# Layer 0 opens with two feature blocks over nine column chunks; w_mod products queue behind the splits

## The chip, the cores and the metric

The kernel runs on one core of one Trainium2 chip. The time is that of one execution on the device, in microseconds (us), and of several executions the median is given.

## What is computed

A trunk of two layers works on 256 tokens with 2048 features. Each layer normalises its input, scales and shifts it by numbers that come from the condition `c` through the matrix `w_mod`, multiplies it by the wide matrix `w_in`, runs retention and latent attention on the pieces, merges them by gates, multiplies by `w_out` and adds the result. Cut to what matters here:

```python
c_act = jax.nn.silu(c)
mod = c_act @ w_mod + b_mod                       # (1, 6144) from a (2048, 6144) matrix, for each layer
shift, scale, gate = jnp.split(mod, 3, axis=-1)
h = rms_norm(x, g_norm) * (1.0 + scale[:, None, :]) + shift[:, None, :]
proj = h @ w_in                                   # (256, 2048) x (2048, D_IN)
```

Everything is in 32-bit floats.

## The kernel before

The 2048 features are 16 blocks of 128, and a block of the normalised, scaled and shifted input `h` lies with its features on the partitions and the 256 tokens along the free axis. A product with a matrix goes in chunks. A chunk is one transfer of 512 KB, two feature blocks by 512 columns. SyncE (SP) issues it into one of five `wst` buffers (`load`, L233). ScalarE (ACT) writes a rounded copy of it and VectorE (DVE) the remainder, into one of three `whl` buffers (`split_into`, L240 to L242). TensorE (PE) then multiplies high by high, high by low and low by high (`chunk`, L262 to L273). A chunk of the first four columns is 24 matmuls of 256 columns, one of the others 12 matmuls of 512. The function `load_split` (L246) does load and split, and gives the split a raised priority for the scheduler, which orders the instructions of each engine's queue.

The numbers `scale` and `shift` come from `w_mod`. Except at the very start VectorE makes these products: for each row block of `w_mod` it multiplies the tile by a column of `cact` and adds it to an accumulator (`mod_rows`, L341 to L346), and TensorE only sums over the partitions at the end (`mod_finish`, L356). A list `background` holds these steps, and `bg` (L417) takes some of them at each `load_split`, by a rate. In `first_products` they go through `mod_pair` with two `ring` buffers, one step for each transfer of 512 KB; later, in `mod_slice`, through the `wst` buffers that the weights use as well.

Layer 0 opens in `start` (L494), whose instructions on TensorE, VectorE and ScalarE stand in an order written by hand. The input comes in four transfers, then 16 transfers of `w_mod` bring scale and shift for the first four feature blocks, first all eight of scale, then all eight of shift, each 256 rows by 512 columns. TensorE transposes the input and multiplies the scale rows (L528); VectorE adds up the shift rows. When both are done `h` is made for four blocks (L541 to L545).

The function `first_products` (L581) then goes over groups of feature blocks, four groups of four in layer 0. In each group it goes over 14 column chunks of 512 (rq and rk, n 0 to 3; rv, n 4 to 7; rg, n 8 to 11; the first gate, n 12 and 13) and adds the group's part to what stands there: the first part is copied out of PSUM by ScalarE (L604), each later one is added by VectorE (L606). Beside a group the background makes scale and shift of the next group. The rate is set such that the last step is taken 8 loads before the group's end (`SPARE`), in layer 1 three loads before (`SPARE1`). At the start of the next group `make_h` turns them into `h`.

Line numbers are those of the kernel before.

## Time and profile before

| | us |
|---|---|
| median of 3 executions | 2107.25 |
| lowest and highest of them | 2105.28, 2107.37 |
| the profiled execution, whole | 2107.54 |
| its span in the profile | 2105.8 |
| TensorE busy | 2045.3 |
| VectorE busy | 1505.9 |
| ScalarE busy | 1060.1 |

The whole time of the profiled execution is 1.7 us longer than its span. A busy engine has an instruction in work; a matmul's end is modelled, so that back-to-back matmuls overlap in the rows. PEclk is TensorE's granted clock, as a share of full speed. DMA is the mean busy share of the 16 DMA engines, GB/s is what they moved.

### The profile page before, as it was taken

What the parts mean: (1) busy time and instruction counts of PE and PEld (TensorE: products, weight loads), DVE (VectorE), ACT (ScalarE), POOL (GpSimd) and SP (SyncE); (2) the same over time, 40 slices, a digit from 0 to 9 for tenths busy, and PEclk for the clock granted to TensorE, in tenths of its full rate; (3) what the DMA queues carried; (4) which work ended last, traced back from release to release, by engine and by line L of the source; (5) the groups of instructions that cost most, each with busy time, mean ns of one, the idle gap of its engine ahead of it and who ended that gap; (6) DMA issues with size and microseconds to landing.
All of it is one profiled execution on the core that took longest, in us unless ns stands there. A gap on an engine that the chain in (4) does not pass through costs nothing. (4 is left out here: it accounts for less than half of the span.)

```text
span 2105.8 us, 31895 instructions
## 1 busy us (share of the span) xinstructions
PE 2045.3 (97%) x12410; PEld 1806.7 (86%) x12414; DVE 1505.9 (72%) x2258; ACT 1060.1 (50%) x1489; POOL 0.2 (0%) x4
## 2 busy tenths in 40 slices
PE   7999999999999999999999999999999999999998
PEld 4887888997789998778999779889878999988887
DVE  5789887777777786666577776557866777765564
ACT  4554355654356665334454454446544666644453
POOL 0000000000000000000000000000000000000000
PEclk9999999999999999999999999999999999999999
DMA  8988866566766667776558976665667666666672
GB/s 315 310 283 274 293 190 199 165 196 228 263 203 194 186 196 250 242 242 216 181 167 304 313 256 184 196 186 156 196 220 231 184 193 186 216 221 189 192 243 91
DMA packets 263511, 460.60 MB, mean 219 GB/s; under 512 B 18464, under 2 KB 68032, under 8 KB 263360
## 3 DMA queue, kind: packets, MB, share of 16 engines
q1 hardware_dynamic: 263360, 458.57, 68.4%
q8 instruction: 97, 1.59, 0.3%
q14 instruction: 54, 0.44, 0.1%
HBM read 456.41 MB, written 2.10 MB: 218 GB/s over the span
## 5 line engine op out<-in xcount | busy, mean ns | idle before, releaser
L241 ACT ACTIVATE whl<-wst 128x1024 fp32r<-128x1024 f32 (+1 forms) x708 | 706.9, 1006 | 770.4 <-PE acc L273 634.9
L242 DVE TENSOR_TENSOR whl<-wst,whl 128x1024 fp32r<-128x1024 f32 (+1 forms) x708 | 811.6, 1156 | 267.2 <-ACT whl L241 264.0
L270 PE MATMUL acc<-whl,h 128*128 128x512 f32 x2048 | 513.6, 391 | 0.9 <-DVE rv L606 0.7
L270 PEld LDWEIGHTS acc<-whl,h 128*128 128x128 f32 x2048 | 381.6, 188 | 79.8 <-issue 1.7
L270 PE MATMUL acc<-h,whl 128*128 128x256 f32 x2432 | 331.0, 287 | 8.6 <-ACT h L241 3.8
L270 PEld LDWEIGHTS acc<-h,whl 128*128 128x128 f32 x2432 | 310.0, 194 | 12.5 <-ACT h L241 5.0
L273 PE MATMUL acc<-whl,h 128*128 128x512 f32 x1024 | 281.8, 395 | 8.5 <-DVE whl L242 8.1
L270 PE MATMUL acc<-whl,z 128*128 128x512 f32 x1024 | 256.7, 392 | 3.8 <-ACT whl L241 3.8
L346 DVE SCALAR_TENSOR_TENSOR macc<-wst,cact,macc 128x512 f32<-128x512 f32 x180 | 135.0, 750 | 140.9 <-DMA wst<-in_w_mod 138.8
L273 PEld LDWEIGHTS acc<-whl,h 128*128 128x128 f32 x1024 | 188.8, 188 | 53.9 <-DVE whl L242 16.9
L270 PEld LDWEIGHTS acc<-whl,z 128*128 128x128 f32 x1024 | 192.8, 189 | 44.7 <-ACT whl L241 4.5
L273 PE MATMUL acc<-h,whl 128*128 128x256 f32 x1216 | 175.1, 284 | 0.0
L273 PEld LDWEIGHTS acc<-h,whl 128*128 128x128 f32 x1216 | 159.1, 193 | 0.1
L273 PE MATMUL acc<-whl,z 128*128 128x512 f32 x512 | 139.8, 395 | 13.2 <-DVE whl L242 13.1
L346 DVE SCALAR_TENSOR_TENSOR tmp<-ring,cact,tmp 128x512 f32<-128x512 f32 x150 | 112.0, 751 | 51.4 <-DMA ring<-in_w_mod 49.9
L273 PEld LDWEIGHTS acc<-whl,z 128*128 128x128 f32 x512 | 95.2, 189 | 39.2 <-DVE whl L242 20.3
L270 PE MATMUL acc<-c,whl 128*128 128x256 f32 x640 | 102.7, 289 | 1.0 <-DVE ma L643 1.0
L270 PEld LDWEIGHTS acc<-c,whl 128*128 128x128 f32 x640 | 86.8, 191 | 1.3 <-ACT q L241 1.2
L270 PE MATMUL acc<-m,whl 128*128 128x256 f32 x512 | 67.3, 283 | 0.0
L270 PEld LDWEIGHTS acc<-m,whl 128*128 128x128 f32 x512 | 64.0, 192 | 0.1
L270 PE MATMUL acc<-whl,m 128*128 128x512 f32 (+1 forms) x256 | 56.5, 365 | 0.0
L273 PE MATMUL acc<-c,whl 128*128 128x256 f32 x320 | 56.0, 283 | 0.0
(259 smaller groups left out, 1889.7 us busy)
## 6 DMA issues: line engine op xcount, KB each, us to landing
wst<-in_w_in SPq DMA_DIRECT2D x416, 512.0 KB, 4.5
wst<-in_w_mod SPq DMA_DIRECT2D x96, 512.0 KB, 4.3
ring<-in_w_mod SPq DMA_DIRECT2D x80, 512.0 KB, 5.5
wst<-in_w_ret_proj SPq DMA_DIRECT2D x64, 512.0 KB, 4.8
wst<-in_w_mla_proj SPq DMA_DIRECT2D x64, 512.0 KB, 4.6
wst<-in_w_out SPq DMA_DIRECT2D x64, 512.0 KB, 3.7
wst<-in_w_ukv SPq DMA_DIRECT2D x32, 512.0 KB, 3.8
wst<-in_w_uq SPq DMA_DIRECT2D x32, 384.0 KB, 4.0
```

Of the source, the lines that this page charges most:

```text
L241: A.activation(hi, src, AF.Copy)
L242: V.tensor_tensor(lo, src, hi.bitcast(F32), ALU.subtract)
L270: T.matmul(o, x, y, start=start and i == 0, stop=False, skip_group_check=True)
L273: T.matmul(o, x, y, start=False, stop=stop, skip_group_check=True)
L346: V.scalar_tensor_tensor(acc, w[:, k, :], cact[:, k0 + k : k0 + k + 1], acc, ALU.mult, ALU.add)
```

## The change

`GROUPS[0]` becomes (0,2), (2,2), (4,4), (8,4), (12,4): the first group of four blocks is cut into two of two. In the new first group only nine of the 14 column chunks are made (`FIRST`), so the second group makes those nine for two blocks and the other five for four. `start` fetches `w_mod` for two blocks only, in eight transfers of 512 rows by 256 columns, scale and shift by turns; behind them the first three chunks of `w_in`, then the eight transfers of `w_mod` for the second two blocks with a chunk of `w_in` after every two. The products of these second blocks become the background of the new first group. The scale products on TensorE stand between the transposes and behind them. `h` is made with the scale inside the activation, and one more VectorE instruction for each block. Everywhere in the kernel the `w_mod` products are queued on VectorE behind the last split that was traced before them (`behind_splits`), and `load` and `mod_fetch` are kept on SyncE in the order of the program. The spare loads are 2, 3, 8, 8, 8 in layer 0 and 3, 3 in layer 1, as before there.

```diff
-GROUPS = ((0, 4), (4, 4), (8, 4), (12, 4)), ((0, 8), (8, 8))
+GROUPS = ((0, 2), (2, 2), (4, 4), (8, 4), (12, 4)), ((0, 8), (8, 8))
+FIRST = 9
-SPARE1 = 3
-SPARE = 8
+SPARE = (2, 3, 8, 8, 8), (3, 3)
 def load(src, nk, n, t=None):
-        DMA.dma_start(v, src.rearrange("(k p) n -> p k n", p=P))
+        tc.keep_in_program_order(DMA.dma_start(v, src.rearrange("(k p) n -> p k n", p=P)))
+    def behind_splits():
+        return tc.issue_after(last_split[-1].ins) if last_split else nullcontext()
 def load_split(src, nk, n, early=False):
-        w = load(src, nk, n)
+        w = loaded.pop(0) if loaded else load(src, nk, n)
-            split_into(hi, lo, w)
+            last_split.append(split_into(hi, lo, w))
 def mod_pair(l, kg, ng, fetched=None):
-                mod_rows(acc[i], mod_fetch(room[used[0] % len(room)], l, kg + 16 * i, k0, ng), k0, nd)
+                if fetched:
+                    w = fetched[i, k0]
+                else:
+                    used[0] += 1
+                    w = mod_fetch(ring()[used[0] % RING], l, kg + 16 * i, k0, ng)
+                with behind_splits():
+                    mod_rows(acc[i], w, k0, nd)
 def mod_slice(l, m0, k0):
-        mod_rows(macc, w, k0, 2)
+        with behind_splits():
+            mod_rows(macc, w, k0, 2)
 def start():
-        ws = {(i, k): mod_fetch(quarter("wmod"), 0, 16 * i, k, ng) for i in (1, 0) for k in range(0, KT, nd)}
+        steps = [(i, k) for k in range(0, KT, nd) for i in (1, 0)]
+        ws = {(i, k): mod_fetch(quarter("wmod"), 0, 16 * i, k, ng) for i, k in steps}
+        loaded.extend(load(src, 2, 512) for src in first[:HP])
+        later = {}
+        for n, (i, k) in enumerate(steps):
+            later[i, k] = mod_fetch(quarter("wmod"), 0, ng + 16 * i, k, ng)
+            if n % 2:
+                loaded.append(load(first[HP + n // 2], 2, 512, quarter("wst") if HP + n // 2 >= WP else None))
+            turns = {4: 0, 6: nd}
             for pair in range(KT // 2):
+                if pair in turns:
+                    scale_rows(turns[pair])
...
             for k0 in range(0, KT, nd):
                 mod_rows(acc, ws[0, k0], k0, nd)
+            prepared.append(load_split(first[0], 2, 512, early=True))
             A.activation(row[0:1, :], pr[0:1, : ng * P], AF.Copy)
+            mod_sum(0, 0, ng, [acc], ones[:, 0:1])
             mod_sum(0, 16, ng, [row[0:1, :]], ones[0:1, 0:1])
             make_amul(0, 0, ng)
...
+                A.activation(hi, xh0[:, k, :], AF.Identity, bias=shift, scale=scale)
+                V.tensor_scalar(xh0[:, k, :], xh0[:, k, :], scale, shift, ALU.mult, ALU.add)
+                V.tensor_tensor(lo, xh0[:, k, :], hi.bitcast(F32), ALU.subtract)
 def first_products(l, hh, r, u, second):
+            if n1 == 2:
+                todo, steps, columns = [second], 9, FIRST
+            else:
+                todo, steps, columns = [mod_pair(l, k, 4) for k in range(k1, k1 + n1, 4)], 17, COLUMNS
-            rate[0] = len(background) / (sum(kg + ng - k for k in upto) // 2 - (SPARE, SPARE1)[l])
-            for n in range(COLUMNS):
+            rate[0] = len(background) / (sum(kg + ng - k for k in upto[:columns]) // 2 - len(prepared) - SPARE[l][i])
+            for n in range(columns):
```

## Rows read from the trace of the kernel before

**Rows 1.** The page, part 1: busy us, share of the span, instructions by engine.
```profile
PE 2045.3 (97%) x12410; PEld 1806.7 (86%) x12414; DVE 1505.9 (72%) x2258; ACT 1060.1 (50%) x1489; POOL 0.2 (0%) x4
```

**Rows 2.** Windows: stretch, length, busy us by engine, PEclk, DMA share, GB/s.
```profile
30.00:40.00 10.00, 6.46 (x25) 3.49 (x24) 9.14 (x18) 2.44 (x4) 0.00 (x0) 0.85 1.05 387
```

**Rows 3.** Timeline of the start: start us, duration us, engine, line, what [idle before].
```profile
19.07 14.27 PE L528 MATMUL aux<-wmod,cact 128*1 128x512 f32 x32
19.18 0.38 ACT L333 ACTIVATE r<-aux 128x256 f32<-128x256 f32 x1 [0.26 <-PE aux L331]
22.02 0.89 ACT L230 ACTIVATE sin_t<-angle,cst 128x256 f32<-128x256 f32 x2
24.33 0.49 DVE L344 TENSOR_SCALAR extra<-wmod,cact 128x512 f32<-128x512 f32 x1 [3.44 <-DMA wmod<-in_w_mod]
35.17 1.06 ACT L241 ACTIVATE whl<-wst 128x1024 fp32r<-128x1024 f32 x1 [1.21 <-DMA wst<-in_w_in]
39.76 3.88 PE L270 MATMUL acc<-h,whl 128*128 128x256 f32 x16 [0.87 <-ACT h L544]
44.53 0.64 PE L270 MATMUL acc<-h,whl 128*128 128x256 f32 x4
```

**Rows 4.** Windows of the groups of layer 0: first, second, third.
```profile
39.70:123.60 83.90, 81.22 (x457) 69.93 (x457) 63.22 (x78) 49.31 (x70) 0.00 (x0) 0.98 0.89 300
123.60:207.40 83.80, 82.17 (x456) 69.74 (x457) 75.03 (x100) 35.48 (x41) 0.00 (x0) 0.98 0.84 275
207.40:288.40 81.00, 79.59 (x457) 67.88 (x456) 73.54 (x96) 34.58 (x38) 0.00 (x0) 1.00 0.84 275
```

**Rows 5.** Timeline, TensorE in the first group: two neighbours of each kind of chunk.
```profile
50.29 2.08 PE L270 MATMUL acc<-h,whl 128*128 128x256 f32 x16
...
53.17 2.08 PE L270 MATMUL acc<-h,whl 128*128 128x256 f32 x16
...
72.87 1.98 PE L270 MATMUL acc<-whl,h 128*128 128x512 f32 x8
...
75.59 1.98 PE L270 MATMUL acc<-whl,h 128*128 128x512 f32 x8
```

**Rows 6.** Waits of the whole span: engine, line, awaited: us, times, longest.
```profile
PE acc L273 <- DVE whl L242: 21.1, 25, 1.8
...
DVE macc L346 <- DMA wst<-in_w_mod: 138.8, 74, 6.3
```

**Rows 7.** Timeline in layer 0's last stage: one product ahead of a split.
```profile
861.00 1.06 ACT L241 ACTIVATE whl<-wst 128x1024 fp32r<-128x1024 f32 x1 [1.52 <-PE acc L273]
862.55 0.75 DVE L346 SCALAR_TENSOR_TENSOR macc<-wst,cact,macc 128x512 f32<-128x512 f32 x1 [1.65 <-DMA wst<-in_w_mod]
863.22 1.22 DVE L242 TENSOR_TENSOR whl<-wst,whl 128x1024 fp32r<-128x1024 f32 x1
864.50 1.20 PE L273 MATMUL acc<-whl,h 128*128 128x512 f32 x4 [1.70 <-DVE whl L242]
```

**Rows 8.** Windows: a stall of TensorE and what follows; rows of 1 KB.
```profile
500.00:516.00 16.00, 10.85 (x46) 8.13 (x46) 13.50 (x28) 4.24 (x6) 0.00 (x0) 0.68 0.71 240
...
2057.00:2058.00 1.00, 1.00 (x6) 0.84 (x5) 1.00 (x1) 0.00 (x0) 0.00 (x0) 1.00 1.01 358
```

**Rows 9.** VectorE by line and shape, 0 to 330 us: count, busy us, mean ns.
```profile
L346 DVE SCALAR_TENSOR_TENSOR tmp<-ring,cact,tmp 128x512 f32<-128x512 f32 x90 | 66.9, 750 | 25.4 <-DMA ring<-in_w_mod 24.7
L606 DVE TENSOR_TENSOR qk<-qk,acc 128x512 f32<-128x512 f32 x24 | 15.6, 684 | 1.4 <-PE acc L273 1.4
...
L545 DVE SCALAR_TENSOR_TENSOR h<-xh,mod,h 128x256 fp32r<-128x256 f32 x4 | 1.7, 483 | 0.6 <-ACT h L544 0.6
```

**Rows 10.** Timeline: last product, first matmul of the second group, a pair of additions.
```profile
108.72 1.54 DVE L346 SCALAR_TENSOR_TENSOR tmp<-ring,cact,tmp 128x512 f32<-128x512 f32 x2 [0.31 <-DMA ring<-in_w_mod]
...
123.65 0.50 PE L270 MATMUL acc<-h,whl 128*128 128x256 f32 x2 [1.48 <-ACT h L241]
...
177.93 1.28 DVE L606 TENSOR_TENSOR rv<-rv,acc 128x512 f32<-128x512 f32 x2
```

More of the change, by code (lines that the diff above doesn't have):

```diff
@@ L230, in rotary_tables, with load @@
             A.activation(sin_t[:, n], a[:, n * S : (n + 1) * S], AF.Sin, scale=cst[:, K_INV + 2 + n : K_INV + 3 + n])
-    def load(src, nk, n):
-        t = wp.tile([P, 1024], F32, name="wst", tag="wst")
+    def load(src, nk, n, t=None):
+        t = wp.tile([P, 1024], F32, name="wst", tag="wst") if t is None else t
         v = t[:, : nk * n].rearrange("p (k n) -> p k n", k=nk)
-        DMA.dma_start(v, src.rearrange("(k p) n -> p k n", p=P))
+        tc.keep_in_program_order(DMA.dma_start(v, src.rearrange("(k p) n -> p k n", p=P)))
         return v
@@ L387, in mod_fetch, with mod_pair @@
         nd = 1024 // n
-        DMA.dma_start(w, w_mod[l, k0 * P : (k0 + nd) * P, m0 * P : m0 * P + n].rearrange("(k p) n -> p k n", p=P))
+        src = w_mod[l, k0 * P : (k0 + nd) * P, m0 * P : m0 * P + n]
+        tc.keep_in_program_order(DMA.dma_start(w, src.rearrange("(k p) n -> p k n", p=P)))
         return w
-    def mod_pair(l, kg, ng):
+    def mod_pair(l, kg, ng, fetched=None):
         acc = [tmp_tile()[:, : ng * P] for _ in range(2)]
@@ L512, in start, with scale_rows @@
             y = rsqrt_small(v, 2)
+            pr = aux_tile()
+            def scale_rows(k0):
+                for k in range(k0, k0 + nd):
+                    T.matmul(pr[0:1, : ng * P], cact[:, k : k + 1], ws[1, k0][:, k - k0, :], start=k == 0, stop=k == KT - 1)
+            turns = {4: 0, 6: nd}
             for pair in range(KT // 2):
+                if pair in turns:
+                    scale_rows(turns[pair])
                 ps = aux_tile()
@@ L524, in start @@
             next(rotary, None)
-            pr = aux_tile()
+            for k0 in range(2 * nd, KT, nd):
+                scale_rows(k0)
             for k0 in range(0, KT, nd):
-                for k in range(nd):
-                    T.matmul(pr[0:1, : ng * P], cact[:, k0 + k : k0 + k + 1], ws[1, k0][:, k, :], start=k0 + k == 0,
-                             stop=k0 + k == KT - 1)
-            for k0 in range(0, KT - nd, nd):
                 mod_rows(acc, ws[0, k0], k0, nd)
+            prepared.append(load_split(first[0], 2, 512, early=True))
             A.activation(row[0:1, :], pr[0:1, : ng * P], AF.Copy)
+            mod_sum(0, 0, ng, [acc], ones[:, 0:1])
             mod_sum(0, 16, ng, [row[0:1, :]], ones[0:1, 0:1])
             make_amul(0, 0, ng)
-            mod_rows(acc, ws[0, KT - nd], KT - nd, nd)
-            for k in range(ng):
-                V.tensor_scalar(xh0[:, k, :], xh0[:, k, :], amul[0][:, k : k + 1], None, ALU.mult)
-            first = [w_in[0, k0 * P : (k0 + 2) * P, n : n + 512] for n in (C_RQ, C_RK) for k0 in range(0, ng, 2)]
-            prepared.append(load_split(first[0], 2, 512, early=True))
-            mod_sum(0, 0, ng, [acc], ones[:, 0:1])
             for k in range(ng):
                 hi, lo = hh.block(k)
-                shift = mods[0][:, k : k + 1]
-                A.activation(hi, xh0[:, k, :], AF.Identity, bias=shift)
-                V.scalar_tensor_tensor(lo, xh0[:, k, :], shift, hi.bitcast(F32), ALU.add, ALU.subtract)
+                scale, shift = amul[0][:, k : k + 1], mods[0][:, k : k + 1]
+                A.activation(hi, xh0[:, k, :], AF.Identity, bias=shift, scale=scale)
+                V.tensor_scalar(xh0[:, k, :], xh0[:, k, :], scale, shift, ALU.mult, ALU.add)
+                V.tensor_tensor(lo, xh0[:, k, :], hi.bitcast(F32), ALU.subtract)
             prepared.extend(load_split(src, 2, 512, early=True) for src in first[1:HP])
-        return r, hh
+        return r, hh, mod_pair(0, ng, ng, later)
     def scaled(l, n):
@@ L589, in first_products @@
         for i, (kg, ng) in enumerate(groups):
-            if l == 0 and i == 1:
+            if l == 0 and i == 2:
                 vectors(1)
@@ L615, in layer @@
         if l == 0:
-            r, hh = start()
+            r, hh, second = start()
         else:
-            hh = Pairs("h")
-        tiles = first_products(l, hh, r, u)
+            hh, second = Pairs("h"), None
+        tiles = first_products(l, hh, r, u, second)
         zz = Pairs("z")
```

13 lines of the change are left out of this document (6 added, 7 removed).

## The prediction, on record before the run

> **What bounds the kernel now.** I read the page's first part, then the windows, the waits, and last the timeline where the windows show a hole. The page's first part says that TensorE is busy 97% of the span [rows 1], so only two kinds of time can be won: time before its main work starts, and stalls in it. The windows show the first: from 30 to 40 us the transfers run at 387 GB/s while TensorE is busy for 6.46 of 10 us [rows 2], and the timeline of the start shows why this is a wait. VectorE's first shift product starts at 24.33, on the landing of the 13th of 20 transfers of 512 KB (four of input, eight of scale, then this first of shift); the first weight chunk, the 21st, is taken up by ScalarE at 35.17; the first main matmul starts at 39.76 [rows 3]. Eight transfers lie between the first two, so one takes (35.17 - 24.33) / 8 = 1.355 us. The start is bound by 8 MB of `w_mod` that stands ahead of the first weight.
>
> The windows of the groups show what comes next. Group one takes 83.9 us with VectorE busy for 63.2, group two 83.8 with VectorE busy for 75.0, group three 81.0 with 73.5 [rows 4]. TensorE sets their length: neighbours of one kind lie 53.17 - 50.29 = 2.88 us apart for the narrow chunk and 75.59 - 72.87 = 2.72 for the wide one [rows 5], so 8 and 20 of them in a group make 23.0 + 54.4 = 77.4 us. But VectorE is a close second.
>
> The waits show the other kind: 25 waits of TensorE, 21.1 us, for the remainder of a split, and 138.8 us in which VectorE stands at a `w_mod` product whose transfer has not landed [rows 6]. The timeline joins the two [rows 7]: ScalarE has the high part ready at 862.06 (861.00 + 1.06). VectorE stands at a product until 862.55, takes it, and makes the remainder only from 863.22; TensorE has waited 1.70 us at 864.50. One case of that kind stands there for the pattern.
>
> **The start.** Four tiles less of scale and four less of shift stand ahead of the first weight: it is the 13th transfer, and lands by about 24.3 us. The tiles have rows of 1 KB instead of 2. The nearest row, a microsecond of the last stage in which only rows of 1 KB move, has 358 GB/s [rows 8] against 387, and eight transfers at that ratio take 0.9 us more; I take 25.2. The Trainium skill, DMA: Bandwidth & Descriptors, Specifications, puts the least transfer for full rate at 512 B; by it the landing would be 24.3. The row is below full rate, so it does not bear this out, though it is no clean test; neither changes what follows.
>
> For a chain on ScalarE now ends later than the landing. `pr` takes one of four PSUM buffers before the transposes, and eight scale matmuls stand between them. The copy of `r` starts at 19.18 now [rows 3]; I add 0.9 us for the lost buffer and 2 x 0.9 us for two groups of four matmuls of 256 columns (an estimate: 32 of 512 columns take 14.27 us now, 0.45 each [rows 3], and half of that is 0.22), so it starts at about 21.9. The rotary tables follow on ScalarE and end at 22.02 + 0.89 = 22.91 now [rows 3], so at 25.7 then. Only then comes the first high part (1.06 [rows 3]), the remainder (1.22 [rows 7]), and by my estimate 0.5 for three short VectorE instructions and 0.6 for the first `h`: 29.1 us, with bounds 27.5 and 31. That is 10.7 us before 39.76.
>
> **The work added to VectorE.** The second two blocks get 32 products of 256 elements, at 0.483 us from the nearest instruction of this length [rows 9]: 15.5 us. Before, their shift part was hidden in the start's wide products, and their scale part on TensorE. The Trainium skill, VectorE: DVE Perf Modes, in the section on the TRN2 errata, speaks against such halves: each instruction has a fixed part, and tiles of 512 or more are advised. The rows agree: 0.750 us for 512 and 0.483 for 256 [rows 9], of which 0.22 is fixed. By its formula, (N + 151) / 0.96 ns, the 32 would take 13.6 us, and VectorE's end below would come some 2 us earlier.
>
> Nine columns are now added once more, two instructions each: 18 x 0.684 [rows 9] = 12.3 us. The second finish has four subtractions of at most 0.483, so 1.9; `h` of two blocks two more of the additions' size, so 1.4. Together 31.1. Neighbours overlap a little (a pair of additions takes 1.28 [rows 10], not 2 x 0.684 = 1.37), which leaves 29 us.
>
> So the opening, up to the first matmul of the third new group (now at 123.65 [rows 10]), has two ends. By TensorE: 29.1 + 77.4, with 1.9 for the slow first chunk (39.76 to 44.53 instead of 2.88 [rows 3, 5]), 1 for sums and 1 to 5 for the boundary between the two new groups: 112. By VectorE: 63.2 + 29 = 92.2 us of work from about 28.4, less 4 that may lag behind the boundary (two columns' additions and half of `h`), plus idle time. In group two it was idle for 83.8 - 75.0 = 8.8 us, in group one for 20.7; I take 4. That gives 120.6. VectorE ends last. Bounds: 115 with no idle time and more lag, 127 with idle time as in group two and 2 us more. Against 123.65 the opening wins 3.1 us. TensorE then stands some 8 us at that boundary, and the clock falls after a stall: in the 16 us around a stall at 505 the granted clock was 0.68 [rows 8], a mix of the two levels of 1.2 and 2.4 GHz. I charge 1.5 us more than for today's 1.48 us wait [rows 10]. The opening nets -1.6 us, with bounds -9 and +9.
>
> **The order edges.** A product behind the last split traced before it is just the reverse of the case above: the 862.06 remainder no longer waits for the landing. What may still stand behind a product is the split of a load that was issued after the product's own, so it has not landed either. This reaches most of the 21.1 us of waits [rows 6], and part of the 16 us around 505, where TensorE is busy for only 10.85 [rows 8]. Not all comes back: the product gives its `wst` buffer free a little later, and SyncE, in order, issues the next loads from that. I take somewhat under half of the 21.1, -9 us; bounds -18 and 0. Loads in program order cost nothing by themselves where the issues go by turns already. The place to name is the third group: the rows of the second layer's vectors need a `tmp` buffer, and all loads of that group now stand behind their issue. It may cost 2 us there, inside the bounds. The spare numbers for layer 1 and the later groups are unchanged, so I cost them at nothing; what hides the finish there is 8 x 2.72 = 21.8 us of loads.
>
> **Sum.** 2107.54 for the profiled execution, less 1.6, less 9: 2096.9; the median lies 0.3 lower. I say 2097.
>
> **Rivals.** First, that VectorE is not the bound in the opening, because its queue has less idle time and the products no longer block it: the start's 10.7 us come through whole, and with the edges' 9 the time is 2088. For it speaks that VectorE was busy for only 63.2 of 83.9; against it that 92 us of work do not go into the 83 us up to 112. Chance 0.15.
>
> Second, that the edges change nothing: what waits is then bound by the loop of five `wst` buffers, and each split moved forward only meets a later transfer. The 138.8 us of waits for `w_mod` speak for it. With the opening's -1.6 the time is 2106. Chance 0.18.
>
> Third, slower: the end of the new second group. Today the last product ends at 110.26 and the first matmul of the next group starts at 123.65 [rows 10]: 13.4 us for finish, sum and `h` through busy queues, with 21.8 us of loads to hide it. Now there are three spare loads, 3 x 2.72 = 8.2 us. If the last product there ends after 110, TensorE loses what the chain has beyond that. With idle time of 8 us, from waits for `ring` transfers as in group two, the products end at 28.4 + 81 + 8 = 117 (81 is the 92.2 less 11 for what follows the last product) and the chain at 131, which is 7 us later than now, and 2 more for the clock: +9. With the edges giving nothing, the time is 2116. Chance 0.22.
>
> **How the numbers follow.** The forecast (opening about even, half of the stalls gone) has 0.45, and its own range is 2088 to 2103. Two tenths of a per cent, 4.2 us, is about what a measurement of this kernel can tell from no change; so faster means below 2103, slower above 2111.5. Faster: 0.45 + 0.15 = 0.60. Within: 0.18. Slower: 0.22. The range goes from 2083 (the whole start and most of the stalls) to 2115 (short of the third rival's end), and leaves out 1 in 10 on each side at most.
>
> **What would show it.** The start is right if the first main matmul stands at 27.5 to 31 and ScalarE's rotary tables end just before the first high part. The VectorE step is right if VectorE is busy for 90 us or more between there and the first matmul of blocks 4 to 7, if that matmul stands near 120, and if TensorE waits for `h` there for several us; it is wrong if that matmul stands at 112 or at 131. The edges are right if the 21.1 us of waits for remainders fall to about 10, with most cases between 850 and 960 gone, and if no product with a wait for its transfer stands ahead of a remainder whose high part was ready. Waits of ScalarE for weight transfers that grow by as much would show the second rival. Changes in stages that have no `w_mod` work would show that the order of the queues was drawn anew, which I have not priced.

## The result and the profile after

The changed kernel takes 2124.05 us (median of 4 runs, 2123.20 to 2124.49) where the kernel before takes 2106.27 on the same chip: a ratio of 1.0084, 95% interval 1.0071 to 1.0098. It is some 18 us slower; the prediction was 2097, 10 us faster, with 2083 to 2115 as its range. The profiled execution took 2123.2 us with a span of 2121.4.

The page's first part after the change (engine, busy us, share of the span, instructions), to be read beside [rows 1]:

```profile
PE 2044.8 (96%) x12417; PEld 1814.7 (86%) x12418; DVE 1538.0 (72%) x2312; ACT 1063.5 (50%) x1494; POOL 0.2 (0%) x4
```

TensorE is busy for as long as before, and the span has grown by 15.6 us (2121.4 against 2105.8): the loss is idle time of TensorE. VectorE has 32.1 us more work, close to the 31.1 that the prediction added up.

To see where the idle time lies, the two traces are laid side by side by work: the columns of all main matmuls are added up in the order in which they start, and the table gives the time at which a share of the total is reached in the kernel before, and how much later (+) or earlier each other kernel reaches it. A column that is flat between two lines loses nothing there. The kernels of the experiments are in it already; "no order" and the other names are explained with them.

```
share  before  after  no order  edges  order  no order  order   edges   order,
               (all)            alone  alone  +4 ring   +4 ring +4 ring rows moved
0.01     60.7   -3.0    -3.5    +0.1   +1.1    -4.4     -4.8    +1.0    -4.1
0.03     97.0  +13.4    +7.8    +1.0   +3.6    +7.5     +8.7    +0.9   +12.5
0.05    141.2  +21.5   +19.8    +1.1   +3.1   +10.5    +11.1    -3.3   +20.3
0.11    255.5  +27.4   +16.8    -1.9   +8.0    +7.5     +8.2    -6.3   +27.0
0.21    460.6  +25.5   +19.0    +0.5   +5.2    +8.5     +5.7    -5.6   +25.0
0.29    638.9  +11.1    +4.7   -13.9   +6.2    -5.9     -8.6   -20.0   +10.6
0.39    857.3  +11.1    +4.4   -14.1   +5.7    -6.1     -8.9   -20.2   +10.7
0.43    944.1   -1.4    -8.1   -26.6   +6.6   -18.7    -21.4   -32.7    -1.9
0.71   1505.1   -2.0    -9.2   -28.2   +5.5   -24.5    -21.3   -38.6    -0.6
0.79   1672.7   -6.7   -14.1   -33.1   +3.1   -29.5    -26.0   -43.5    -5.5
0.81   1718.4   -2.4   -13.9   -32.9   +3.1   -29.2    -23.2   -43.3    -5.3
0.85   1811.5   +3.1   -14.6   -33.7   +8.5   -30.0    -18.4   -44.0    -5.8
0.89   1890.0  +12.2   -14.6   -33.6  +17.0   -29.9     -9.5   -43.9    -5.7
0.95   2000.2  +12.2   -14.6   -33.6  +16.9   -29.9     -9.5   -44.0    -5.7
0.99   2076.6  +15.7   -14.6   -33.6  +20.4   -29.9     -5.8   -44.0    -2.2
```

The column "after" has three parts. It loses 25 us by 460 us, in the opening. It wins 27 us between 460 and 945, where layer 0's later stages have modulation slices as background. It loses about 22 us between 1673 and 2077, in layer 1, where the prediction expected nothing.

**The opening.** The timeline of its start (start us, duration us, engine, line, what, idle before) answers [rows 3]:

```profile
24.40 0.39 ACT L337 ACTIVATE r<-aux 128x256 f32<-128x256 f32 x1
27.24 0.89 ACT L230 ACTIVATE sin_t<-angle,cst 128x256 f32<-128x256 f32 x2
28.04 1.04 ACT L241 ACTIVATE whl<-wst 128x1024 fp32r<-128x1024 f32 x1
...
24.82 0.69 DVE L442 TENSOR_TENSOR xh<-xT,r 128x512 f32<-128x512 f32 x1 [8.39 <-ACT r L337]
25.43 0.35 DVE L348 TENSOR_SCALAR extra<-wmod,cact 128x256 f32<-128x256 f32 x1
25.81 7.77 DVE L350 SCALAR_TENSOR_TENSOR extra<-wmod,cact,extra 128x256 f32<-128x256 f32 x15
33.50 1.22 DVE L242 TENSOR_TENSOR whl<-wst,whl 128x1024 fp32r<-128x1024 f32 x1
...
33.73 1.93 PE L356 MATMUL aux<-ones,extra 128*128 128x1 f32 x8 [5.92 <-DVE extra L350]
36.74 3.63 PE L274 MATMUL acc<-h,whl 128*128 128x256 f32 x13 [1.08 <-ACT h L565]
```

VectorE's instructions run in the order written in `start`. It stands idle for 8.39 us until ScalarE's copy of `r`, then normalises, and only then makes the 16 shift products, whose weights have been landing meanwhile: they end at 33.6, and TensorE waits 5.92 us for them. It then sums them over the partitions (1.93 us), and from the sums ScalarE makes `h`. For that the first main matmul waits, which starts at 36.74; the remainder of the first weight, ready at 34.72, is not what holds it.

The windows from there to the first matmul of blocks 4 to 7, and of layer 0's last stage (stretch, length, busy us by engine, granted clock, DMA share, GB/s), answer [rows 4]:

```profile
36.70:144.40 107.70, 89.39 (x469) 73.53 (x469) 88.60 (x136) 51.95 (x74) 0.00 (x0) 0.93 0.68 235
...
850.00:1000.00 150.00, 150.00 (x745) 124.59 (x744) 107.49 (x123) 66.10 (x73) 0.00 (x0) 1.00 0.76 253
```

TensorE is idle for 18.3 of the 107.7 us and VectorE for 19.1; the transfers move 235 GB/s where group one had 300 [rows 4]. Nothing is full. In the second stretch TensorE is busy all the time.

The waits of the whole span (engine, line, awaited: us, times, longest) answer [rows 6]:

```profile
PE acc L274 <- ACT whl L241: 32.8, 19, 7.0
...
PE acc L277 <- DVE whl L242: 2.0, 1, 2.0
...
DVE macc L350 <- DMA wst<-in_w_mod: 0.2, 1, 0.2
...
ACT whl L241 <- DMA wst<-in_w_in: 163.1, 73, 6.8
```

The 21.1 us of waits for remainders are gone, and so are VectorE's 138.8 us at products without their data: the edges (each product queued behind the last split) do what they say. In their place TensorE waits 32.8 us for the high part (4.3 in the kernel before), because ScalarE waits for weights that have not landed. The timeline of the end of the first group and of the second (SyncE's queue, then ScalarE, then TensorE) shows why:

```profile
46.04 0.37 SPq L237 DMA_DIRECT2D wst<-in_w_in  x1
71.43 0.37 SPq L393 DMA_DIRECT2D ring<-in_w_mod  x1
...
87.13 0.37 SPq L393 DMA_DIRECT2D ring<-in_w_mod  x1
87.59 0.42 SPq L237 DMA_DIRECT2D wst<-in_w_in  x1
91.38 0.37 SPq L393 DMA_DIRECT2D ring<-in_w_mod  x1
91.84 0.42 SPq L237 DMA_DIRECT2D wst<-in_w_in  x1
...
92.36 1.06 ACT L241 ACTIVATE whl<-wst 128x1024 fp32r<-128x1024 f32 x1 [4.31 <-DMA wst<-in_w_in]
96.67 1.06 ACT L241 ACTIVATE whl<-wst 128x1024 fp32r<-128x1024 f32 x1 [3.25 <-DMA wst<-in_w_in]
...
93.47 2.11 PE L274 MATMUL acc<-whl,h 128*128 128x512 f32 x8 [1.97 <-ACT whl L241]
97.78 2.14 PE L274 MATMUL acc<-whl,h 128*128 128x512 f32 x8 [1.30 <-ACT whl L241]
```

In program order each weight load follows one ring load, and goes out half a microsecond behind it (87.13 and 87.59, 91.38 and 91.84). The ring load waits for one of two buffers, which a product gives free; the product is queued behind splits; the splits wait for weights. The engines go in step, one pair of loads in about 4 us. Ahead of this the queue stands still altogether: SyncE issues nothing from 46.41 to 71.43, 25.0 us. The third ring load is next there, and the buffer that it needs is freed by the first products of the second group, which end at 71.4. Without the order (the first experiment) ten weight loads go out from 39.07 to 66.72 instead.

**The late loss.** The wait of SyncE's queue at the row load of 1876 us, and the timeline of SyncE's queue, ScalarE and TensorE around it:

```profile
SPq L372 <- DVE part L367: 14.4, 1, 14.4
```
```profile
1860.58 0.37 SPq L237 DMA_DIRECT2D wst<-in_w_mod  x1
1876.48 0.34 SPq L372 DMA_DIRECT2D tmp<-in_b_mod  x1
1876.87 10.42 SPq L237 DMA_DIRECT2D wst<-in_w_in  x7
...
1883.21 1.06 ACT L241 ACTIVATE whl<-wst 128x1024 fp32r<-128x1024 f32 x1 [5.10 <-DMA wst<-in_w_in]
...
1884.32 3.78 PE L274 MATMUL acc<-whl,h 128*128 128x512 f32 x8 [7.00 <-ACT whl L241]
```

SyncE issues nothing for 15.5 us (1860.58 + 0.37 to 1876.48). At its head stands the load of a row of `b_mod`, which needs a `tmp` buffer (14.4 us of the wait end with VectorE's part of a finish, L367, and 1.0 with the matmuls that read it, L377); seven weight loads stand behind it and go out in one burst. TensorE waits 7.00 us, and its next eight matmuls take 3.78 us where eight of that kind take 1.98 [rows 5]; the granted clock of the 8 us from 1884 is 0.74, a mix of the two levels of 1.2 and 2.4 GHz. In the table the column "order alone" steps at the same shares of work (0.85 and 0.89) as the column "after".

### The profile page after: what moved, and what is told of

Read it like the earlier page. It is cut to its first block, busy times and chain, and to the rows that moved or that the text cites. A ratio compares the mean times of both kernels' runs of the same rounds, so it can differ in the third digit from the quotient of the medians.

```text
span 2121.4 us, 31949 instructions
## 1 busy us (share of the span) xinstructions
PE 2044.8 (96%) x12417; PEld 1814.7 (86%) x12418; DVE 1538.0 (72%) x2312; ACT 1063.5 (50%) x1494; POOL 0.2 (0%) x4
## 4 chain that ended last, share of the span: by engine, by line
PE 86%; DMA 6%; DVE 5%; ACT 2%; issue 1%; SPq 0%; ACTq 0%; DVEq 0%
PE acc L274 52%; PE acc L277 26%; DMA wst<-in_w_in 5%; ACT whl L241 1%; DVE whl L242 1%; DVE tmp L350 1%; PE aux L266 1%; PE aux L264 1%; PE aux L265 1%; PE acc L265 1%; PE acc L266 1%; PE acc L264 1%; PE aux L893 0%; DMA ring<-in_w_mod 0%; DVE extra L350 0%
## 5 line engine op out<-in xcount | busy, mean ns | idle before, releaser
L274 PE MATMUL acc<-h,whl 128*128 128x256 f32 x2432 | 335.0, 289 | 15.0 <-ACT whl L241 7.3
L274 PEld LDWEIGHTS acc<-h,whl 128*128 128x128 f32 x2432 | 314.3, 197 | 18.6 <-ACT whl L241 7.6
L274 PE MATMUL acc<-whl,z 128*128 128x512 f32 x1024 | 254.8, 390 | 1.3 <-ACT whl L241 1.2
L277 PE MATMUL acc<-h,whl 128*128 128x256 f32 x1216 | 177.7, 287 | 2.0 <-DVE whl L242 2.0
L277 PEld LDWEIGHTS acc<-h,whl 128*128 128x128 f32 x1216 | 161.4, 196 | 2.2 <-DVE whl L242 2.2
L277 PE MATMUL acc<-whl,z 128*128 128x512 f32 x512 | 137.3, 390 | 0.1
L277 PEld LDWEIGHTS acc<-whl,z 128*128 128x128 f32 x512 | 95.8, 188 | 20.2 <-DVE whl L242 0.5
```

Of the source, the lines that this page charges most:

```text
L274: T.matmul(o, x, y, start=start and i == 0, stop=False, skip_group_check=True)
L277: T.matmul(o, x, y, start=False, stop=stop, skip_group_check=True)
```

## The experiments

Three theories stood at the outset. A: the program order is the loss (a load that waits for its buffer holds back all loads behind it). B: the opening is the loss. C: the edges put the products, and so the buffers, late. All ratios below are to the kernel before, measured on the same chip.

**1. No order.** The changed kernel with the two `keep_in_program_order` taken away:

```diff
-        tc.keep_in_program_order(DMA.dma_start(v, src.rearrange("(k p) n -> p k n", p=P)))
+        DMA.dma_start(v, src.rearrange("(k p) n -> p k n", p=P))
-        tc.keep_in_program_order(DMA.dma_start(w, src.rearrange("(k p) n -> p k n", p=P)))
+        DMA.dma_start(w, src.rearrange("(k p) n -> p k n", p=P))
```

> The changed kernel without its program order: both kinds of load (weights of the products, modulation weights) are left to the scheduler; opening, first columns and the edges behind the splits stay. Theory A (the order is the loss: a modulation load that waits for its buffer holds back the weight loads that follow it in the queue, in the groups up to 165 us, and row loads of b_mod do the same around 1780 and 1876): the late loss of about 22 us goes, and of the 25 us lost by 150 us at least 15 go; 2075 to 2090 us. Theory B (the opening itself is the loss: a late first h, a short first group, the finish chain at its end): only the late 22 us go, the lag at 150 us stays above +15; 2098 to 2106 us. Theory C (the edges alone put the products, and with them the buffers, late): as B here, and the next kernel shows the lag without the order.

Measured: 2092.28 us, ratio 0.9931 (0.9910 to 0.9952). The order costs the changed kernel 2124.05 - 2092.28 = 31.8 us. In the table, by the last line, "after" and "no order" lie 30.3 apart: 23 of these come behind the share of 0.79 (1672.7 us) and 6.5 ahead of 0.21 (460 us). So theory A holds for the late loss, but not for the opening, of which 19.0 us stay. The time itself came out between the two expectations, because both parts count. The waits of TensorE around the two boundaries of the opening show what remains:

```profile
65.91 0.18 PE L356 MATMUL aux<-ones_h,part 128*128 128x1 bf16 x1 [1.97 <-ACT part L366]
...
71.25 4.21 PE L274 MATMUL acc<-h,whl 128*128 128x256 f32 x18 [2.46 <-ACT h L241]
...
134.60 0.19 PE L356 MATMUL aux<-ones_h,part 128*128 128x1 bf16 x1 [7.45 <-ACT part L366]
...
144.67 3.80 PE L274 MATMUL acc<-h,whl 128*128 128x256 f32 x18 [1.35 <-ACT h L241]
```

The window from the first main matmul to that of blocks 4 to 7:

```profile
35.30:144.60 109.30, 87.00 (x469) 74.56 (x469) 89.84 (x137) 53.37 (x76) 0.00 (x0) 0.87 0.79 261
```

There are now two boundaries at which a chain (last product, finish, sum, `h`) runs while TensorE has nothing else: from about 64 to 71.25, and from 127 to 144.67. The kernel before has one such boundary up to blocks 4 to 7, with a wait of 1.48 us [rows 10]. The two kernels reach the third group at nearly the same time in different ways: with the order TensorE is slowed all through the second group, without it TensorE is 5.4 us behind the kernel before at 117 us and then waits at the group's end.

**2. The edges alone.** The kernel before, with its old opening and free loads, and the one addition that each modulation product is queued behind the last split traced:

```diff
+    def behind_splits():
+        return tc.issue_after(last_split[-1].ins) if last_split else nullcontext()
...
-            split_into(hi, lo, w)
+            last_split.append(split_into(hi, lo, w))
...
-        mod_rows(macc, w, k0, 2)
+        with behind_splits():
+            mod_rows(macc, w, k0, 2)
```

> The kernel before with one part of the change alone: modulation products queued behind the latest split on VectorE (in the groups and in the later slices); old opening, no program order. Theory A: the gain seen in layer 0 between 460 and 945 us (about 28 us) is the edges' own; 2075 to 2085 us. Theory C: the products come late, buffers come free late, and the groups lose what the changed kernel loses; 2100 to 2125 us. Rival D (the edges gain only together with loads in program order): 2100 to 2107 us, with the waits for remainders as in the kernel before.

Measured: 2073.66 us, ratio 0.9842 (0.9822 to 0.9861): 33 us faster than the kernel before. That is 1.3 us below theory A's range; theory C and rival D fall. The table says where: nothing by 460 us, 14 us from there to 639, 12.5 between 857 and 944, 5 between 1505 and 1673. The waits of the whole span have one line left of what was 21.1 us:

```profile
PE acc L277 <- DVE whl L242: 2.9, 4, 1.3
```

**3. The order alone,** on the kernel before:

```diff
-        DMA.dma_start(v, src.rearrange("(k p) n -> p k n", p=P))
+        tc.keep_in_program_order(DMA.dma_start(v, src.rearrange("(k p) n -> p k n", p=P)))
...
+        tc.keep_in_program_order(DMA.dma_start(w, src.rearrange("(k p) n -> p k n", p=P)))
```

> The kernel before with program order of the loads alone; old opening, no edges. Theory A: the late stalls of about 22 us appear, and loads stand behind ring loads in the groups; 2120 to 2145 us. Theory B: the order costs nothing by itself; 2104 to 2110 us.

Measured: 2128.14 us, ratio 1.0103 (1.0085 to 1.0120), 21 us slower. That is inside theory A's range. Of its waits, two lines:

```profile
ACT whl L241 <- DMA wst<-in_w_in: 142.9, 72, 6.8
...
PE acc L270 <- ACT whl L241: 22.0, 13, 6.6
```

ScalarE's waits for `w_in` (14.7 us in the kernel before, 142.9 here; 163.1 in the changed kernel, 4.6 there without order) are the order's. In the old opening they cost 5 us, in layer 1 some 17.

**4. Order in the opening only.** As the first experiment, but the loads issued ahead of the hand-written schedule stay ordered (`load` and `mod_fetch` call `in_order`):

```diff
+    opening = [True]
+    def in_order(ins):
+        return tc.keep_in_program_order(ins) if opening[0] else ins
...
+        opening[0] = False
```

> The changed kernel with program order kept only for the loads of the opening (16 pieces of the two modulation groups and the first seven weights), free behind it. Theory A: within 8 us of the kernel without any order (2075 to 2095 us), since nothing in the opening waits for a buffer. Theory B: 2098 to 2106 us. If the order of the opening's loads is itself worth something, this is faster than the kernel without any order by 2 us or more.

Measured: 2093.76 us, ratio 0.9936 (0.9919 to 0.9952), the same as without any order, within the noise. The opening's loads need no fixed order, and it does not harm them: SyncE's queue shows no wait there.

These four split the change: edges -33.1, opening +18.6 (the first less the second: 2092.28 - 2073.66), order +31.8. That the three add up to the change (+17.3, and +17.8 was measured) is no test, since each is the difference of one kernel to the next. The size of a part depends on the others: the order costs 21.4 us by itself and 31.8 on top of the rest.

**5. Which edges.** The kernel before with edges on the slices' products (`macc`) alone; against the second experiment:

```diff
                 w = mod_fetch(room[used[0] % len(room)], l, kg + 16 * i, k0, ng)
-                with behind_splits():
-                    mod_rows(acc[i], w, k0, nd)
+                mod_rows(acc[i], w, k0, nd)
```

> The kernel before with the edges of the later slices alone (the products that run between 460 and 1000 us and again from 1550 us); the products of the groups are free again, old opening, no program order. Theory A (the edges gain where a full group of products is no longer due, as the times of equal matmul work of the run with all edges say: 0.5 us lost by 460 us, 28 us gained by 983 us, 34 by 1770 us): 2070 to 2078 us. Rival: the groups' edges carry a part (21 us of remainder waits were predicted to be theirs as well): 2080 to 2092 us.

Measured: 2071.88 us, ratio 0.9840 (0.9818 to 0.9862), the same as with all edges. The groups' edges give nothing that can be measured, so that the gain is that of the slices' edges.

**6. The row in its own place.** The changed kernel, order and all; a row of `b_mod` goes straight into the gate row:

```diff
-        b, n = tmp_tile(), m0 - 32
+        n = m0 - 32
...
+        b = gate_row[n // 8][:, n % 8 * P : n % 8 * P + 512]
-        V.tensor_tensor(gate_row[n // 8][:, n % 8 * P : n % 8 * P + 512], ps, b, ALU.add)
+        V.tensor_tensor(b, ps, b, ALU.add)
```

> The changed kernel, order and all; only the rows of b_mod for layer 1's gate are loaded straight into the gate row's own buffer, where they waited for a shared scratch buffer. Theory A (a weight load pinned behind a row load whose buffer is not free is what stalls TensorE near 1780 and 1880 us): the waits of 3.9 and 7.0 us for split weights go with the slow clock behind them; 2100 to 2111 us. Rival: the modulation slices' own loads, pinned as well, hold the queue at those places: 2119 to 2126 us.

Measured: 2114.43 us, ratio 1.0036 (1.0020 to 1.0052): 9.6 us off the changed kernel, 3 us short of the expectation. Near 1880 the stall is gone, its row load has no wait there. Near 1780 it is not: the row that opens a new gate row still waits, now for that buffer, as the waits of SyncE's queue say:

```profile
SPq L375 <- DVE v L242: 10.7, 1, 10.7
```

So the loss goes with the wait of the row load, not with the kind of buffer. A step of 5 us between 1189 and 1248, by the times of equal work, took back some of it; its cause is open.

**7. Rows on another queue.** The changed kernel, order and all, with the four row loads issued by GpSimd:

```diff
-        DMA.dma_start(b, b_mod[l, m0 * P : m0 * P + 512].unsqueeze(0).broadcast_to([P, 512]))
+        nc.gpsimd.dma_start(b, b_mod[l, m0 * P : m0 * P + 512].unsqueeze(0).broadcast_to([P, 512]))
```

> The changed kernel, order and all; only the four row loads of b_mod for layer 1's gate are issued from GpSimd's queue, where nothing stands behind them. Theory A (a weight load pinned behind a waiting row load is the late loss): the times of equal matmul work of the changed kernel against the one without order step by 4.0, 6.3, 9.0 and 4.5 us behind 1666, 1762, 1855 and 2012 us; all four steps go, 24 us in sum, and 2098 to 2105 us. Rival (the pinned slice loads hold the queue): 2115 to 2125 us.

Measured: 2106.49 us, ratio 0.9995 (0.9985 to 1.0004): 17.6 us off, 1.5 short of the expectation. Between 1640 and 1960 us the windows of the changed kernel and of this one are:

```profile
1640.00:1960.00 320.00, 306.76 (x2034) 282.92 (x2034) 214.43 (x352) 171.46 (x289) 0.00 (x0) 0.97 0.61 188
```
```profile
1640.00:1960.00 320.00, 319.19 (x2123) 293.71 (x2123) 224.91 (x364) 179.55 (x299) 1.61 (x3) 1.00 0.67 200
```

TensorE's idle time falls from 13.2 to 0.8 us. Three of the four steps (4.0, 6.3 and 9.0 us) are gone; the last, 4.5 us near 2020, stays. There TensorE's own instructions stand in another order (24 transposes with waits of 1.8 and 1.1 us ahead of the first matmuls of `w_out`, where the kernel without order does them between the matmuls); what orders them so was not tried.

**8. Four ring buffers, without order and with it.** `RING = 4` in the kernel of the first experiment, and in the changed kernel:

> The changed kernel without program order and with four ring buffers for modulation weights instead of two. Theory R (the products of blocks 4 to 7 end late, at 138 us, since each ring load waits for its buffer): the products end by 128 us, the wait at the end of the second group falls from 17 us to 10 or less, and 2082 to 2087 us. Rival (transfers or VectorE's own work bound that group; 35 weight tiles of 512 KB and some 60 us of VectorE work in 73 us): the wait stays above 14 us, 2089 to 2096 us.

> The changed kernel, order and all, with four ring buffers instead of two. Theory H (in the groups, weight loads stand in SyncE's queue behind ring loads that wait for a buffer): with two more buffers a ring load rarely waits, the lag against the kernel before at 460 us falls from +25.5 to +14 or less, and 2104 to 2114 us (the late stalls stay). Rival (the ordered loads follow one another in any case, and the lag comes from VectorE): above +20 at 460 us, 2118 to 2125 us.

Measured: 2077.09 us without order (ratio 0.9863, 0.9843 to 0.9883), 2103.61 with it (0.9985, 0.9976 to 0.9995): two buffers more are worth 15.2 and 20.4 us. By the table both kernels have the same lag at 460 us, +8.5 and +5.7: with four buffers the order costs nothing in the groups. Without order, the window from the first main matmul to that of blocks 4 to 7:

```profile
35.70:135.00 99.30, 84.78 (x469) 72.18 (x470) 88.14 (x134) 53.60 (x76) 0.00 (x0) 0.93 0.87 296
```

Against the first experiment VectorE's work is nearly the same (88.1 us against 89.8), its idle time is 11.2 us instead of 19.5, and blocks 4 to 7 begin at 135.05 instead of 144.67. The last product of that group ends at 124.7, and TensorE waits 8 us at the group's end instead of 17, as theory R says. By the times of equal work 10.5 of the 15.2 us lie ahead of 460 us and the rest in layer 1's groups, between 1150 and 1248; with the order nearly all of it lies ahead of 460. The time with order is just under the expected 2104 to 2114, and that without is 5 us better than expected.

**9. Both causes of the order's cost away:** order, four ring buffers, rows on GpSimd's queue.

> The changed kernel with program order, four ring buffers and the row loads on GpSimd's queue. If the two kinds of waiting load (ring loads in the groups, row loads in layer 1) are all that the order costs: 2077 to 2084 us, within 7 us of the kernel with four ring buffers and no order (2077.1). Rival (the order costs something else besides): 2088 us or more.

Measured: 2087.95 us, ratio 0.9902 (0.9885 to 0.9918). It falls between the two expectations, at the edge of the rival's: against the kernel with four buffers and no order (2077.09), 10.9 us of the order's cost are left. The times of equal work place 7 us of them between 1113 and 1132 us, in layer 1's first group, and about 4 near 2020. In the first place TensorE waits 1.9 and 2.0 us for parts of splits that the kernel without order has ready. SyncE's queue waits there for `wst` buffers, up to 8.0 us, and for ring buffers at most 1.0 us at a time, so it is not a ring load that holds it; what makes the difference was not tried.

**10. Shift products first.** The kernel without order; half of the shift products written ahead of the normalisation:

```diff
+            for k0 in range(0, KT // 2, nd):
+                mod_rows(acc, ws[0, k0], k0, nd)
             for k in range(0, ng, 2):
                 normalise(xh0[:, k : k + 2, :], k, r)
...
-            for k0 in range(0, KT, nd):
+            for k0 in range(KT // 2, KT, nd):
                 mod_rows(acc, ws[0, k0], k0, nd)
```

> The changed kernel without program order, and in the opening half of the shift products written ahead of the normalisation on VectorE. Theory S (the first h is late because 16 products wait behind the normalisation): the first main matmul moves from 35.4 to about 31 us. If TensorE carries this through, 2086 to 2089 us. Rival (VectorE or the ring sets the end of the second group, whatever its start): the start moves, the first matmul of blocks 4 to 7 stays within 2 us of 144.7, and 2090 to 2095 us.

Measured: 2087.55 us, ratio 0.9913 (0.9889 to 0.9937). The timeline of TensorE:

```profile
28.68 1.14 PE L356 MATMUL aux<-ones,extra 128*128 128x1 f32 x8 [1.89 <-DVE extra L350]
30.90 5.33 PE L274 MATMUL acc<-h,whl 128*128 128x256 f32 x21 [1.08 <-ACT h L567]
...
138.27 4.20 PE L274 MATMUL acc<-h,whl 128*128 128x256 f32 x18 [1.35 <-ACT h L241]
```

The first main matmul moves from 35.37 to 30.90, and blocks 4 to 7 from 144.67 to 138.27. Theory S holds, and TensorE carries it through: the first main matmul is 4.5 us earlier and the time 4.7 us shorter.

**11. What is left of the opening.** Three mends together (shift products first, four ring buffers, no order, and layer 1's vectors one group later); the same with one more spare load; and the same with the sums of blocks 2 to 7 taken from the fp32 products directly, without the two copies and two subtractions of the finish:

> The changed kernel without program order, mended in three places: shift products ahead of the normalisation, four ring buffers, and the transposition of layer 1's vectors moved behind one more group (its row loads ended a wait of 3.6 us at 135 us). If the mends add up (4.7 us, 15.2 us, and up to 3.6 us): 2066 to 2071 us, under the kernel with the edges alone. Rival (they hide the same wait at the end of the second group): 2073 to 2077 us.

> As the mended kernel, with the products of blocks 2 and 3 spread so that three loads of the first group are left behind them instead of two. If the wait of 6.6 us at the first boundary (64 to 70 us) is set by the last product and the chain behind it: that wait falls to 4 us or less, 1 to 3 us faster than the mended kernel. Rival (the transfers set when those products can run): no difference beyond 1 us.

> The mended kernel (no order, shift products first, four ring buffers, vectors one group later); the sums of the modulations of blocks 2 to 7 are taken from the fp32 products directly, as the opening does it, without the two copies and two subtractions that split them. Theory F (the chain from the last product to h stands open at both ends of the short groups): the wait of about 7 us at 59 to 66 us falls to 4 or less and that at 123 to 131 us by 2 us or more; 2068 to 2072 us. Rival (the products themselves end too late, VectorE being full from 72 to 110 us): the chain's saving is lost to later products, 2073 to 2076 us.

Measured: 2074.92 us (ratio 0.9850, 0.9827 to 0.9873), 2076.42 (0.9856, 0.9837 to 0.9875) and 2071.93 (0.9826, 0.9811 to 0.9841). The mends do not add up: 4.7 and 15.2 us apart, 17.4 together, with the vectors' move in it. That they hide part of the same wait, as the rival says, fits the sum but is not shown by itself. The spare load gives no gain (1.5 us slower, at the edge of the noise). The shorter chain gives 3.0 us. Blocks 2 to 3 and 4 to 7 begin, in the mended kernel and then with the short chain:

```profile
66.39 4.21 PE L274 MATMUL acc<-h,whl 128*128 128x256 f32 x18 [2.44 <-ACT h L241]
...
130.93 1.22 PE L274 MATMUL acc<-h,whl 128*128 128x256 f32 x4 [4.29 <-ACT h L241]
```
```profile
63.73 2.67 PE L274 MATMUL acc<-h,whl 128*128 128x256 f32 x18 [2.49 <-ACT h L241]
...
127.56 1.23 PE L274 MATMUL acc<-h,whl 128*128 128x256 f32 x4 [4.28 <-ACT h L241]
```

At the first boundary TensorE's last chunk ends at 58.6 in the mended kernel and at 60.5 with the short chain, so 7.8 us between the groups become 3.3, as theory F says. At the second the wait for `h` is 4.3 in both, where 2 us less were expected. So the chain is a part of what is left, and the rest of the 8 to 11 us to the next kernel is not taken apart further.

**12. Old opening, edges, four ring buffers.**

> The kernel before with all the edges and with four ring buffers; old opening, no program order. Theory R (the ring binds only in the short second group of the new opening, since the old first group has 76 us of TensorE work for the same 24 us of products): 2070 to 2077 us, as with two buffers. Rival (the ring binds in every group): 2058 to 2068 us, and then the new opening is still the slower one by 10 us or more.

Measured: 2063.73 us, ratio 0.9794 (0.9775 to 0.9814), the fastest kernel of the study, 43 us under the kernel before and 60 under the changed one. Theory R falls: the ring binds with the old opening too, 10 us against the edges alone. In the table 6 of these lie ahead of 460 us, in layer 0's groups, and 4 between 944 and 1505, in layer 1's. From the first main matmul to blocks 4 to 7 this kernel and, for comparison, the mended new opening need:

```profile
39.70:122.50 82.80, 81.02 (x459) 70.15 (x459) 63.00 (x81) 49.88 (x70) 0.00 (x0) 0.97 0.91 315
```
```profile
29.20:130.90 101.70, 86.03 (x468) 72.50 (x468) 89.11 (x137) 53.42 (x76) 0.00 (x0) 0.93 0.93 311
```

The mended opening starts 11.5 us earlier (29.23 against 40.69), has 26.1 us more VectorE work, and comes to the same point 8.5 us later. So the earlier start, even where it comes as predicted, is more than lost by that point; how much of this the added VectorE work and the second boundary each cost is not shown.

## Why the prediction was wrong, step by step

**The start** was predicted at 29.1 us (27.5 to 31) and came at 36.74. The failing step is the chain from the first high part to `h`: the prediction has the remainder, three short VectorE instructions and `h` follow at once. The tables and the high part came 2.3 us late (28.04 instead of 25.7). But VectorE was not free: 16 products of about half a microsecond stood behind the normalisation in the written order, and the split behind them, so that the remainder started at 33.50, 4.4 us after the high part was ready. What the first matmul waits for is not even the remainder: it is `h`, behind TensorE's sums of these products, 1.93 us that this chain does not count. The prediction counted which data had landed and did not follow VectorE's own order to the end. With half of the products moved, 30.90 was measured, inside the predicted bounds.

**The VectorE step** had the right amount and the wrong idle time. 92.2 us of work (88.2 without what may lag) were predicted, 88.6 measured. The sum allowed 4 us of idle time, and 19.1 were measured; with the start 7.6 us later, 120.6 + 7.6 + 15.1 = 143.3, and blocks 4 to 7 came at 144.47, later than the 131 that was named as the sign of the third rival. Some 8 us of the idle time are the two ring buffers': without order it is 19.5, and with four buffers 11.2. The other 7 above the predicted 4 are not explained. As the prediction said it could, the place is **the third rival's**: the end of the second new group, with ring waits and three spare loads. Its price was +9 us; in the kernel without order the wait there is 17 us, and there is one at the first boundary, 7 us, for which the forecast had 1 to 5.

**The edges** were predicted at -9 us, bounds -18 and 0, and gave -33. The mechanism was right; the size was not. The forecast took somewhat under half of the 21.1 us of TensorE's waits for remainders. Of these 18.2 went. Between 440 and 990 us all waits of TensorE for other engines fall from 20.2 us to 1.7 with the edges alone. The same matmuls in the kernel before and with the edges alone:

```profile
440.00:990.00 550.00, 529.41 (x3269) 467.00 (x3268) 402.85 (x648) 276.31 (x430) 0.00 (x0) 0.99 0.70 222
```
```profile
440.50:962.25 521.75, 520.00 (x3269) 465.38 (x3268) 406.92 (x648) 277.72 (x430) 0.00 (x0) 1.00 0.73 234
```

They take 28.2 us less: 18.8 us of TensorE's idle time and 9.4 us of its busy time. The stretch from 460 to 639 us, with the stall at 505, gave 14 of them. The granted clock explains some 5 us: it was 0.68 in the 16 us around 505 [rows 8], which is 5.1 us short of full speed, and 1.00 from 440 to 500 and from 516 to 990, so that the other waits of this stretch had no slow clock behind them. The other 4 us of busy time are not explained. The forecast and its bound of -18 had counted waits only. The second rival fell: ScalarE's waits for weights did grow, as was named for its sign, but by the order; with the edges alone they are 2.9 us for `w_in`, where the kernel before has 14.7.

**"Loads in program order cost nothing by themselves"** is the step that decides the sign. It cost 21.4 us on the kernel before and 31.8 within the change. The prediction had looked at whether loads go by turns already, not at what stands at the head of the queue when it stops. It named the one mechanism, a row load that needs a `tmp` buffer with all loads behind it, but only for layer 1's vectors in the third group; the four rows of `b_mod` for layer 1's gate, issued on the same queue, cost 19 us by the three steps that went with the seventh experiment (17.6 by its time), and the order costs 6.5 in the groups with two ring buffers and nothing with four. What it costs near 2020 us (4.5) and, with four buffers, in layer 1's first group (7) stays open.

Together: the sum of -1.6 and -9 became +18.6 and -33.1, and +31.8 for the term that was left at nothing. Without the order the time is 2092.28, 5 us from the forecast and inside its range, but that nearness is luck: the opening cost 20 us more than forecast, the edges gave 24 us more, and the two errors cancel.

## What to carry to other kernels

To keep loads in program order makes one queue of them: before it is done, go through every transfer issued on that queue, small rows too, and ask what its buffer waits for, because every load behind it waits for that as well. A group that is cut into two has two chains from the last background product to the next operand, and each needs work of TensorE to hide it; count the chain, the buffers of the background's ring and the shorter work that covers it before counting the earlier start. Where an engine's instructions stand in a written order, follow that order to the instruction that the estimate is about, and not the landing of its data alone. A wait of TensorE that is taken away can give more than its length: here 18.8 us of idle time gave 28.2.

## What the runs showed of the hardware

Transfers of modulation weights in rows of 1 KB moved 348 GB/s in the opening, and transfers of `w_in` in rows of 2 KB right behind them 388, as these two windows of the changed kernel show. The third is of the kernel before, where the modulation weights come in rows of 2 KB:

```profile
14.00:22.00 8.00, 6.54 (x22) 2.86 (x23) 1.30 (x7) 4.05 (x8) 0.00 (x0) 1.00 1.09 348
24.00:27.00 3.00, 3.00 (x16) 1.17 (x15) 2.07 (x5) 2.97 (x6) 0.00 (x0) 1.00 1.05 388
```
```profile
12.00:24.00 12.00, 9.65 (x36) 4.88 (x35) 3.83 (x13) 10.38 (x19) 0.00 (x0) 0.86 1.05 389
```

But for a few packets of 4 B, only packets of 1 KB move in the first window and only packets of 2 KB in the two others. It is the test that the prediction had only one microsecond for [rows 8]: the transfer engines are as busy and move a tenth less, and it is not the matrix that makes the difference. The Trainium skill, DMA: Bandwidth & Descriptors, Specifications, puts the least transfer for full rate at 512 B; here the measurement differs and decides. The row loads on GpSimd's queue took 0.54 us each to issue (three of them, the first of the four 0.67) where SyncE's took 0.34, and cost nothing that can be seen.

Products that follow one another on one accumulator start further apart than those that go by turns to two. The 15 of the opening, shown above, take 7.77 us, 0.52 each; these six of the same shape, from the first group, go by turns to two accumulators and take 0.41 each:

```profile
41.09 2.46 DVE L350 SCALAR_TENSOR_TENSOR tmp<-wmod,cact,tmp 128x256 f32<-128x256 f32 x6
```

The instruction itself is as long in both (0.485 and 0.48 us); what differs is whether the next one overlaps it. In the whole changed kernel, with the accumulators read from the program's order of VectorE's queue, a product that comes right behind one on the same accumulator starts 0.52 us after it with 256 elements (14 pairs) and 0.78 with 512 (89 pairs), and behind one on the other accumulator 0.40 (23 pairs) and 0.66 (median of 7 pairs). Of the 89 pairs 46 are of the slices, where the transfers are less busy than in the opening, so full transfers are not the reason.
